# Ten stores of activation forms moved behind the seam of two products, and the three accumulation chains of a unit given their banks in another order

## The chip, the core and the metric

The kernel runs on one core of one Trainium2 chip. The metric is the device time of the program in microseconds (us): the median of several runs. The engines are PE (TensorE; its weight loads are shown as PEld), DVE (VectorE), ACT (ScalarE), POOL (GpSimd) and SP, whose queue issues nearly all DMAs. Each engine runs its instructions in their program order.

## The reference

One residual block for 512 tokens of width 2048, all in float32. What matters here is the MLP at its end:

```python
h2 = rmsnorm(x, g_mlp[l])
u = jax.nn.relu(jnp.einsum('bsd,df->bsf', h2, w_up[l]))     # 2048 -> 8192
x = x + jnp.einsum('bsf,fd->bsd', u * u, w_down[l])         # 8192 -> 2048
return rmsnorm(x, g_final)
```

Ahead of it stand an input projection, sixteen attention heads of two kinds and an output projection, which the change does not touch.

## The kernel before

Each float32 operand of a matmul is split into a high part (`hi`, a rounding cast on ACT, L63) and a low part (`lo`, a subtraction on DVE, L64); a product is hi x hi + hi x lo + lo x hi. Both products of the MLP are done block by block with seven block products in place of eight, numbered 1 to 7; sums and differences of blocks are formed on DVE.

**First product** (class `Unit`). `w_up` is worked through in 32 units of 256 columns. A unit has seven products of 16 matmuls each: eight that are 512 wide (L687) and eight that are 256 wide (L689). They accumulate in three PSUM chains of one bank each: A takes products 1, 6, 7 and 4, one on top of the other, B takes product 2, and C takes 5 and then 3. In the profile the chains are `psa`, `psb` and `psc`. After products 1, 6 and 7 ACT copies A out (L693, tiles `s`), and the next product of chain A waits for that copy. DVE adds chain B or C to a copy (L706 for B, L703 for C after product 7, L712 for C after product 3), and reads A once more after product 4 (L709 on ACT, L710 on DVE). From these come the unit's results, the tile `c`: two 256-wide halves by L700, relu and square by L714 and L715. Each unit's products 4 and 3 are issued among the next unit's.

The pool of the chains has two buffers for each of three tags, six banks in all. The tags get their banks in the order of their first use. When the first product is over, the pool is closed and two pools take the same six banks: the double-bank accumulators `accd` of the second product get the first four (the first accumulator the two banks of the first tag, the second those of the second tag), and `M1[1]` the last two.

**Stores.** Every two units share one tile `c`. Its seven forms are split and stored to DRAM (`store_form`, tiles `st`, 512 KB each, L722); four of them need one more DVE step first (L570 to L576). The list `todo` takes seven of them whenever a pair is done, and gives one back behind some of the products. Units 30 and 31 are not stored as forms: `store_last` stores their two parts each as they are (tiles `su`, L730). The buffers of `st` and `su` are a ring of three, which later serves for the residual (`xr`) too. What is left of `todo` after the last unit, and the four of `store_last`, are the list `jobs`.

**Second product** (`second`, `load_b`, `load_uf`). `w_down` is worked through in eight groups of units (the first two have three units each, the others four), each in two column halves `db`, each with seven products in the order 1, 5, 2, 6, 3, 7, 4. A product of the first group has 18 matmuls, 512 wide (L96 to L98): a split of 1024 columns (`wd` to `wh` and `wl`, or to `wx`) serves 12 of them, one of 512 columns six. Product 1 accumulates over all groups in `M1`; each other product ends in an accumulator `accd`, which ACT copies out in the first group (L786) and DVE adds to the sums `m` in the others (L788). The weights' blocks are combined on DVE first (L763 to L769). Product 1 of the first group is issued before the last unit's products 4 and 3.

The order on the engines is made when the program is built, by a scheduler that works with priorities and its own estimate of time: it moves an instruction ahead of others that would wait. `tc.issue_after(x)` forbids that an instruction is put ahead of `x`. Without it, the stores of `jobs`, which stand in the second group in the code, were put far ahead, between 1447 and 1465 us in the profile.

Of the kernel before, what the change touches and what calls it, by code (L numbers as in the profile page):

```python
# [8 lines left out]
F32 = mybir.dt.float32  # L9
# [5 lines left out]
P = 128  # L15
NT = 512
# [10 lines left out]
NU = DFF // P // 2  # L27
# [11 lines left out]
def block_kernel(ctx, tc, x, g_attn, w_in, b_f, g_out_sb, g_out_fox, w_out, g_mlp, w_up, w_down, g_final, y):  # L39
# [19 lines left out]
    lows, casts, loads = [None], [None], [None]  # L59
# [120 lines left out]
    with (  # L180
# [17 lines left out]
        def accumulate_v(c0, m, steps, prepare=None, more=None):  # L198

            per = NT // m  # L200
            banks = [acc.tile([P, NT], F32, tag="acc", name="accv") for _ in range(2 if more is not None else TB // per)]
            if more is not None:
                banks += [more.tile([P, NT], F32, tag="more", name="accm") for _ in range(2)]
            ps = [banks[t // per][:, t % per * m:(t % per + 1) * m] for t in range(TB)]
            k1, held = 0, []
            for j, step in enumerate(steps):
                k0, k1 = k1, k1 + step
                if prepare is not None:
                    prepare(k0, step)
                w = load_w([w_in[k0 * P:(k0 + step) * P, c:c + m // len(c0)].rearrange("(a p) c -> p a c", p=P) for c in c0],  # L210
                           step, m)
                held += [(k0 + i, w[i]) for i in range(step)]
                if prepare is None and j == len(steps) - 2:
                    continue
                for t in range(TB):
                    ts = slice(t * P, (t + 1) * P)
                    for k, wk in held:
                        mm3(ps[t], hH[:, k, ts], hL[:, k, ts], *wk, k == 0 and t % per == 0, k == KC - 1)
                    yield len(held) * 3 * (m / 2400 + 0.0133)
                held = []  # L220
            return ps

        def all_of(steps):
            while True:
                try:
                    next(steps)
                except StopIteration as e:
                    return e.value

        def out_product(n, mixed):  # L230
            ps = [acc.tile([P, NT], F32, tag="acc", name="acco") for _ in range(TB)]
            held = []
            for k0 in range(0, 2 * NH, 2):
                e0 = order[k0]
                w = load_w(w_out[e0 * P:(e0 + 2) * P, n * NT:(n + 1) * NT].rearrange("(a p) c -> p a c", p=P), 2, NT)
                ms = []
                for i in range(2):
                    ms.append(u_tile((k0 + i) % 4))
                    split(*ms[i], mixed[k0 // NH][:, (k0 + i) % NH, :])
                held += [(k0 + i, ms[i], w[i]) for i in range(2)]  # L240
                if n == 0 and k0 == 0:
                    continue
                for t in range(TB):
                    ts = slice(t * P, (t + 1) * P)
                    for k, m, wk in held:
                        mm3(ps[t], m[0][:, ts], m[1][:, ts], *wk, k == 0, k == 2 * NH - 1)
                    yield len(held) * 3 * 0.2267
                held = []
            return ps
# [131 lines left out]
        def v_columns(h):  # L381
            return 2 * WSB + h * P if h < NH else o0 + 2 * WSB + (h - NH) * P

        with tc.tile_pool(name="tr0", bufs=2, space=PSUM) as trp:
# [35 lines left out]
            ps = all_of(accumulate_v([v_columns(order[0])], 2 * P + NH, [1, 1] + [2] * 7, prepare, trp))  # L420
# [28 lines left out]
        with tc.tile_pool(name="attp", bufs=1, space=PSUM) as atp:  # L449
# [72 lines left out]
            for i in range(2 * NH):  # L522
                a = HEAD_AT[i]
                c = a + TURN + WEIGH if i != 2 * NH - 2 else VALUES_END + 3
# [28 lines left out]
    def form_parts(p, n):  # L553
        pair = F[p][n // 2][:, 2 * (n % 2):2 * (n % 2) + 2]
        return pair[:, :, 0, :], pair[:, :, 1, :]
# [25 lines left out]
    for n in range(4):  # L581
# [3 lines left out]
        ps = all_of(out_product(n, mixed)) if n else first_ps  # L585
# [38 lines left out]
    ups = ups_cm.__enter__()  # L624
# [11 lines left out]
    class Unit:  # L636
        def __init__(self, u):
            self.u = u
            first, last = (up_rows[i][:, :, 2 * u * P:2 * (u + 1) * P] for i in range(2))

            def blocks():
                return rw.tile([P, 2, KC // 2, P], F32, tag="rw", name="wu")

            def wide(src):
                raw = rw.tile([P, KC // 2, 2 * P], F32, tag="rw", name="wu")
                sp.dma_start(raw, src)
                return [raw[:, :, j * P:(j + 1) * P] for j in range(2)]

            if u == 0:
                b11, t1 = (wp.tile([P, KC // 2, P], F32, tag="wraw", name="wq") for _ in range(2))  # L650
                r = blocks()
                t2, t3 = r[:, 0], r[:, 1]
            else:
                r, q = blocks(), blocks()
                b11, t2, t1, t3 = r[:, 0], r[:, 1], q[:, 0], q[:, 1]
            sp.dma_start(b11, first[:, :, :P])
            self.raw = u not in early
            if self.raw:
                sp.dma_start(t1, first[:, :, P:])
                sp.dma_start(t3, last[:, :, P:])  # L660
                sp.dma_start(t2, last[:, :, P:])
            else:
                for t_, j in ((t1, 0), (t2, 2), (t3, 1)):
                    sp.dma_start(t_, td[u][:, j])
            b21, b22 = wide(last)
            self.b = {1: b11, 5: t1, 6: t2, 2: b21, 7: t3, 3: b22, 4: b21}
            self.A, self.B, self.C = (ups.tile([P, NT], F32, tag=c, name=f"ps{c}") for c in "abc")

        def product(self, p):
            if p == 2:  # L670
# [72 lines left out]
    def load_uf(p, group):  # L743
        uf[p] = form.tile([P, 2, group[1], 2 * P], F32R, tag=f"fh{UF_AT[p]}", name=f"uf{p}")
        sp.dma_start(uf[p].bitcast(F32), ufd[group][p])
# [67 lines left out]
    todo, sg = [], []  # L813
    old = None
    for u in range(NU + 1):
        new = Unit(u) if u < NU else None
        if u == NU - 1:
            for p in ORDER:
                load_uf(p, GROUPS[0])
            b_first = load_b(GROUPS[0], 0)  # L820
        if new is None:
            second(1, b_first, 0, GROUPS[0][1], True)
        for i, (who, p) in enumerate(((new, 1), (old, 4), (new, 5), (new, 6), (old, 3), (new, 2), (new, 7))):
            if who is None:
                continue
            who.product(p)
            if u == 0 and p == 6:

                for q in (4, 3):
                    a_form(q, hr, form_parts(q, 3), s12)  # L830
                xp_cm.__exit__(None, None, None)
                hx = ctx.enter_context(tc.tile_pool(name="hx", bufs=1, reuse_waits="tile"))
                more_parts.append(lambda: parts_at(hx, "hx"))
                sg_cm = tc.tile_pool(name="sg", bufs=1, reuse_waits="tile")
                sg.append(sg_cm.__enter__())
            if todo and i in (0, 2, 4, 5):
                store_form(*todo.pop(0))
            if p == 3 and who.u % 2 == 1 and who.u < NU - 2:
                todo += [(q, who.pair, who.u - 1) for q in A_ORDER]
        old = new  # L840
# [30 lines left out]
    jobs = [lambda a=a: store_form(*a) for a in todo] + [lambda u=u, h=h: store_last(u, h) for u in range(2) for h in range(2)]  # L871
    pieces = [(p, db) for db in range(2) for p in (2, 3, 7, 4)]
    spare = None
    for g, group in enumerate(GROUPS):
        last = g == len(GROUPS) - 1
        for db in range(2):
            if last and db == 1:
                in_w = lambda shape, name: wp.tile(shape, F32R, tag="wraw", name=name)
                last_hidden(0, in_w, in_w)
                last_weights(0, [lambda shape, name, i=i: spare.tile(shape, F32R, name=name) for i in range(2)])  # L880
            b = b_first if g + db == 0 else load_b(group, db)
            for i, p in enumerate(ORDER):
                if g + db + i:
                    second(p, b, db, group[1], g == 0)
                if db == 1 and not last:
                    load_uf(p, GROUPS[g + 1])
                if g == 1 and jobs and i % 2 == 0:
                    jobs.pop(0)()
                if g > 1 and pieces and i == 2:
                    add_residual(*pieces.pop(0))  # L890
        if g == 1:
            sg_cm.__exit__(None, None, None)
            spare = ctx.enter_context(tc.tile_pool(name="spare", bufs=1, reuse_waits="tile"))
# [105 lines left out]
```

## Time and profile before

| what | value |
|---|---|
| median of 3 runs | 2080.35 us (2078.67 to 2081.86) |
| profiled execution: time, span | 2080.91 us, 2079.2 us |
| granted clock of PE, mean | 0.998 |
| first product's units | from about 816 to 1452 us |
| seam of the two products | about 1437 to 1455 us |
| second product | to about 2031 us |

A profile's timeline row gives the start, the duration, the engine, the line in the kernel, the operation and its tiles, and in square brackets how long the engine sat idle before it and what it waited for. Matmuls are pipelined: one that is 512 wide is shown with 0.39 us, while the next starts 0.23 us after it. What a stretch costs is therefore read from starts. In a list of waits the three numbers are the sum in us, how often, and the longest.

### The profile page before, as it was taken

What the parts mean: (1) busy time and instruction counts of PE and PEld (TensorE: products, weight loads), DVE (VectorE), ACT (ScalarE), POOL (GpSimd) and SP (SyncE); (2) the same over time, 40 slices, a digit from 0 to 9 for tenths busy, and PEclk for the clock granted to TensorE, in tenths of its full rate; (3) what the DMA queues carried; (4) which work ended last, traced back from release to release, by engine and by line L of the source; (5) the groups of instructions that cost most, each with busy time, mean ns of one, the idle gap of its engine ahead of it and who ended that gap; (6) DMA issues with size and microseconds to landing.
All of it is one profiled execution on the core that took longest, in us unless ns stands there. A gap on an engine that the chain in (4) does not pass through costs nothing.

```text
span 2079.2 us, 26762 instructions
## 1 busy us (share of the span) xinstructions
PE 2055.9 (99%) x10292; PEld 1747.6 (84%) x10292; DVE 1601.8 (77%) x1827; ACT 1072.2 (52%) x1426; POOL 57.0 (3%) x77
## 2 busy tenths in 40 slices
PE   9999999999999999999999999999999999999998
PEld 8888888888888887888888888887888888888886
DVE  5747748748756657788988988989689989888885
ACT  6334334444446556566666666666644444443433
POOL 0000000001100000000000000000000000000003
PEclk9999999999999999999999999999999999999999
DMA  7947948937833445577778778778756764764732
GB/s 238 300 128 258 303 136 266 315 109 251 288 102 102 148 136 187 182 263 263 243 251 268 246 256 263 239 255 311 283 198 220 261 237 164 269 234 131 274 108 81
DMA packets 356575, 455.88 MB, mean 219 GB/s; under 512 B 11440, under 2 KB 255200, under 8 KB 347360
## 3 DMA queue, kind: packets, MB, share of 16 engines
q1 hardware_dynamic: 355488, 452.05, 65.7%
q10 hardware_dynamic: 960, 2.13, 0.3%
q8 instruction: 81, 1.33, 0.2%
q14 instruction: 46, 0.38, 0.0%
HBM read 347.17 MB, written 106.95 MB: 218 GB/s over the span
## 4 chain that ended last, share of the span: by engine, by line
PE 83%; DVE 7%; DMA 6%; issue 3%; ACT 1%; SPq 0%; DVEq 0%; ACTq 0%
PE accd L96 8%; PE accd L97 8%; PE accd L98 8%; PE psa L687 7%; PE accq L96 5%; PE accq L98 5%; PE accq L97 5%; PE psa L689 4%; PE psc L687 3%; DMA wu<-in_w_up_dram 3%; PE acco L97 3%; PE acco L98 3%; PE acco L96 3%; PE accv L96 3%; PE accv L97 2%
## 5 line engine op out<-in xcount | busy, mean ns | idle before, releaser
L63 ACT CAST wh<-wraw 128x1024 fp32r<-128x1024 f32 (+2 forms) x133 | 135.5, 1019 | 193.5 <-PE accq L97 114.8
L63 ACT CAST wh<-wd 128x1024 fp32r<-128x1024 f32 (+1 forms) x136 | 135.1, 1000 | 178.7 <-PE accd L98 120.6
L64 DVE TENSOR_TENSOR wl<-wraw,wh 128x1024 fp32r<-128x1024 f32 (+2 forms) x133 | 157.7, 1186 | 79.2 <-ACT wh L63 79.0
L64 DVE TENSOR_TENSOR wl<-wu,wh 128x1024 fp32r<-128x1024 f32 x166 | 202.0, 1223 | 15.8 <-PE psa L689 5.4
L63 ACT CAST wh<-wu 128x1024 fp32r<-128x1024 f32 x166 | 172.0, 1049 | 70.7 <-PE psa L687 26.1
L96 PE MATMUL accq<-hH,wh 128*128 128x512 f32 x512 | 201.1, 393 | 0.0
L98 PE MATMUL accq<-hH,wl 128*128 128x512 f32 x512 | 200.0, 391 | 0.0
L97 PE MATMUL accq<-hL,wh 128*128 128x512 f32 x512 | 199.7, 390 | 0.0
L64 DVE TENSOR_TENSOR wl<-wd,wh 128x1024 fp32r<-128x1024 f32 (+1 forms) x136 | 155.8, 1156 | 43.5 <-ACT wh L63 43.3
L96 PE MATMUL accd<-wh,uf 128*128 128x512 f32 x436 | 170.3, 391 | 3.2 <-DVE c L710 2.2
L98 PE MATMUL accd<-wh,uf 128*128 128x512 f32 x436 | 170.4, 391 | 0.0
L97 PE MATMUL accd<-wl,uf 128*128 128x512 f32 x436 | 170.3, 391 | 0.0
L63 ACT CAST wx<-wd 128x1024 fp32r<-128x1024 f32 (+1 forms) x88 | 87.7, 1000 | 121.7 <-PE accd L98 80.2
L64 DVE TENSOR_TENSOR wx<-wd,wx 128x1024 fp32r<-128x1024 f32 (+1 forms) x88 | 101.0, 1155 | 23.4 <-ACT wx L63 23.3
L98 PEld LDWEIGHTS accq<-hH,wl 128*128 128x128 f32 x512 | 96.1, 188 | 20.1
L97 PEld LDWEIGHTS accq<-hL,wh 128*128 128x128 f32 x512 | 96.2, 188 | 19.2
L96 PEld LDWEIGHTS accq<-hH,wh 128*128 128x128 f32 x512 | 96.2, 188 | 19.0
L788 DVE TENSOR_TENSOR m<-m,accd 128x1024 f32<-128x1024 f32 x84 | 102.4, 1219 | 10.8 <-PE accd L98 10.7
L97 PE MATMUL accd<-wx,uf 128*128 128x512 f32 x284 | 110.5, 389 | 0.0
L98 PE MATMUL accd<-wx,uf 128*128 128x512 f32 x284 | 110.5, 389 | 0.0
L96 PE MATMUL accd<-wx,uf 128*128 128x512 f32 x284 | 110.3, 389 | 0.0
L687 PE MATMUL psa<-fl,wh 128*128 128x512 f32 x388 | 105.9, 391 | 1.8 <-DVE fl L64 1.8
(288 smaller groups left out, 4860.8 us busy)
## 6 DMA issues: line engine op xcount, KB each, us to landing
ufd<-st SPq DMA_DIRECT2D x98, 512.0 KB, 6.1
wd<-in_w_down_dram SPq DMA_DIRECT2D x48, 1024.0 KB, 6.5
wraw<-in_w_in_dram SPq DMA_DIRECT2D x84, 512.0 KB, 5.0
uf<-ufd SPq DMA_DIRECT2D x42, 1024.0 KB, 7.0
sums<-in_w_up_dram SPq DMA_DIRECT2D x72, 512.0 KB, 6.0
td<-sums SPq DMA_DIRECT2D x24, 1536.0 KB, 8.0
wu<-td SPq DMA_DIRECT2D x71, 512.0 KB, 5.0
wu<-in_w_up_dram SPq DMA_DIRECT2D x32, 1024.0 KB, 7.5
```

The lines of the kernel that those rows point to most:

```text
L63: ins = casts[0] = act.copy(hi, src)
L64: lows[0] = dve.tensor_tensor(lo, src, hi.bitcast(F32), op=ALU.subtract)
L96: pe.matmul(out, sh, mh, start=first, stop=False, skip_group_check=True)
L97: pe.matmul(out, sh, ml, start=False, stop=False, skip_group_check=True)
L98: pe.matmul(out, sl, mh, start=False, stop=last, skip_group_check=True)
L687: pe.matmul(ps, hi[:, a, :], both, start=a == 0 and p in (1, 2, 5), stop=False, skip_group_check=True)
L689: pe.matmul(ps[:, :2 * P], lo[:, a, :], F[p][a // 4][:, a % 4, 0, :], start=False, stop=a == KC // 2 - 1, skip_group_check=True)
L788: dve.tensor_tensor(M[p][:, :, db, :], M[p][:, :, db, :], ps, op=ALU.add)
```

## The change

```diff
-            self.A, self.B, self.C = (ups.tile([P, NT], F32, tag=c, name=f"ps{c}") for c in "abc")
+            self.B, self.C, self.A = (ups.tile([P, NT], F32, tag=c, name=f"ps{c}") for c in "bca")
...
-            if todo and i in (0, 2, 4, 5):
+            if todo and u < NU - 1 and i in (0, 2, 4, 5):
                 store_form(*todo.pop(0))
...
-                if g == 1 and jobs and i % 2 == 0:
-                    jobs.pop(0)()
+                if g == 0 and jobs and db + i:
+                    with tc.issue_after(casts[0].ins), tc.issue_after(lows[0].ins):
+                        jobs.pop(0)()
```

It has three parts. The chains take their banks in the order B, C, A: chain A's banks go from 0 and 1 to 4 and 5, B's from 2 and 3 to 0 and 1, C's from 4 and 5 to 2 and 3. The last unit (`u` = 31) and the round behind it no longer store forms; of the last pair's seven forms six are left, so that `jobs` has ten stores where it had five. And `jobs` is worked off in the first group of the second product, one store behind each product from the second on (six in the first half, four in the second), where it was worked off in the second group. Each store's cast and subtraction now may not be put ahead of the cast and subtraction of the split that stands before it in the code.

The scheduler makes another order of it at the seam; behind the first group the order is the same again. Three places show it.

On PE, where the second product begins (its first matmul writes `m_0`, which is `M1[0]`); `fh_5662` and `fl_5663` are the forms that product 7 of the last unit reads, `fh_5652` and `fl_5653` those of product 2. With - and + as before and now:

```order
+L687 MATMUL psb<-fh_5652,wh 128x512 x4
+L687 MATMUL psb<-fl_5653,wh 128x512 x4
 L689 MATMUL psb<-fh_5652,wl 128x256 x4
 L689 MATMUL psb<-fl_5653,wl 128x256 x4
 L96 MATMUL m_0_6832<-wh,uf_12525 128x512
+L687 MATMUL psa<-fh_5662,wx 128x512 x4
+L687 MATMUL psa<-fl_5663,wx 128x512 x4
+L689 MATMUL psa<-fh_5662,wx 128x256 x4
+L689 MATMUL psa<-fl_5663,wx 128x256 x4
 L97 MATMUL m_0_6832<-wl,uf_12525 128x512
 L98 MATMUL m_0_6832<-wh,uf_12525 128x512
```

Product 7 stood behind 13 of the 18 matmuls of `m_0` and now stands behind the first of them; product 6 moves too, from behind product 2's 512-wide matmuls to ahead of the end of product 3 of unit 30.

On ACT, at the same place, before. `st` is a store's cast, `wd` a split of the second product, `wu` one of the first; the two copies from `psa` are those behind the last unit's products 6 and 7:

```order
L63 CAST st<-c 128x512 [waits DMAHW0_49,DVE_49]
L63 CAST st<-c 128x512 [waits DMAHW1_49]
L63 CAST wh<-wd 128x512 [waits DVE_49,PE_49]
L63 CAST st<-c 128x512 [waits DMAHW4_49]
L63 CAST wh<-wu 128x1024 [waits DVE_49,PE_49]
L693 COPY s_12642<-psa 128x512 [waits PE_49]
L714 ACTIVATE c<-c 128x1024 [waits DVE_49]
L715 ACTIVATE c<-c 128x1024 [waits Activation_49]
L63 CAST wx<-wu 128x1024 [waits PE_49]
L63 CAST wh<-wd 128x1024 [waits DVE_49]
L693 COPY s_12719<-psa 128x512 [waits DVE_49]
```

And now:

```order
L63 CAST wh<-wd 128x1024 [waits DMAHW6_49,PE_49,Activation_49]
L63 CAST wh<-wd 128x512 [waits PE_49]
L693 COPY s_12633<-psa 128x512 [waits PE_49]
L63 CAST wh<-wu 128x1024 [waits DVE_49,PE_49,Activation_49]
L714 ACTIVATE c<-c 128x1024 [waits DVE_49]
L715 ACTIVATE c<-c 128x1024 [waits Activation_49]
L63 CAST wx<-wu 128x1024 [waits PE_49]
L693 COPY s_12701<-psa 128x512 [waits DVE_49]
L63 CAST wh<-wd 128x1024 [waits PE_49]
L63 CAST wh<-wd 128x512 [waits PE_49]
L63 CAST st<-c 128x512 [waits DMAHW1_49]
```

Three stores' casts have left the stretch, and the copy behind product 7 stands directly behind one cast instead of two.

On ACT in the first group, now (the stores' casts wait for a buffer of the ring, DMAHW, and the copies L786 free an accumulator):

```order
L63 CAST st<-c 128x512 [waits DMAHW4_49,DVE_49]
L63 CAST wh<-wd 128x512 [waits PE_49,Activation_49]
L786 COPY m_12913<-accd 128x2x512 [waits PE_49]
L63 CAST wh<-wd 128x1024 [waits DMAHW0_49,Activation_49]
L63 CAST st<-c 128x512 [waits DMAHW6_49,DVE_49]
L63 CAST wx<-wd 128x512 [waits PE_49,Activation_49]
L63 CAST su<-c 128x512 [waits DMAHW0_49]
L786 COPY m_12945<-accd 128x2x512 [waits PE_49]
```

Before, this stretch held splits and copies alone. On DVE the stores' subtractions and the four extra steps move along with the casts: of the eight stores that stood between the first store of the last pair and L710, one is left. L703 behind the last unit's product 7 stood behind two splits, and now stands behind one. On SP's queue the stores stand among the loads of `wd` for the first group's second half and for the second group.

## The prediction

> **What bounds the kernel now.** The first view is the page's part 1.
>
> ```profile
> PE 2055.9 (99%) x10292; PEld 1747.6 (84%) x10292; DVE 1601.8 (77%) x1827; ACT 1072.2 (52%) x1426; POOL 57.0 (3%) x77
> ```
>
> PE is busy for all but 23.3 us of the 2079.2 us span, so a change that leaves PE's work as it is can only win PE's pauses and the stretches in which its clock is low. The next view, busy time in stretches, shows whether there are any where the change works: the two rows around the seam between the first product and the second, and the one behind them.
>
> ```profile
> 1393.00:1420.00 27.00, 26.82 (x156) 23.52 (x155) 22.23 (x28) 16.17 (x21) 0.00 (x0) 1.00 0.92 296
> 1420.00:1455.00 35.00, 31.13 (x171) 26.36 (x170) 32.78 (x42) 23.05 (x32) 0.00 (x0) 1.00 0.89 317
> 1455.00:1500.00 45.00, 45.00 (x193) 37.04 (x193) 30.71 (x32) 27.83 (x33) 0.00 (x0) 0.96 0.75 266
> ```
>
> The columns are the stretch, its length, the busy time of PE, PEld, DVE, ACT and POOL, PE's granted clock, the DMA share and GB/s. From 1420 to 1455 PE lacks 3.87 us while DVE has work for 32.78 of 35 us; behind it the clock is 0.96. This seam holds a sixth of all of PE's idle time. What ended those pauses is in the list of PE's waits:
>
> ```profile
> PE accd L96 <- DVE c L710: 2.2, 1, 2.2
> PE psa L687 <- ACT s L693: 1.6, 2, 1.4
> PE psc L687 <- DVE s L703: 0.3, 1, 0.3
> ```
>
> Three results that others deliver late: a copy on ACT, and two additions on DVE. PE's timeline places them, and gives what they cost in starts rather than in busy time.
>
> ```profile
> 1426.28 1.09 PE L687 MATMUL psa<-fh,wh 128*128 128x512 f32 x4
> ...
> 1429.07 1.09 PE L687 MATMUL psc<-fh,wh 128*128 128x512 f32 x4
> ...
> 1437.43 0.40 PE L96 MATMUL m<-wh,uf 128*128 128x512 f32 x1
> ...
> 1437.90 0.39 PE L98 MATMUL m<-wh,uf 128*128 128x512 f32 x1
> ...
> 1440.18 0.39 PE L96 MATMUL m<-wh,uf 128*128 128x512 f32 x1
> 1440.53 1.19 PE L687 MATMUL psa<-fh,wx 128*128 128x512 f32 x4
> ...
> 1446.16 1.19 PE L687 MATMUL psa<-fh,wh 128*128 128x512 f32 x4 [1.40 <-ACT s L693]
> ...
> 1449.46 1.20 PE L687 MATMUL psc<-fh,wx 128*128 128x512 f32 x4 [0.26 <-DVE s L703]
> ...
> 1454.74 0.50 PE L96 MATMUL accd<-wh,uf 128*128 128x512 f32 x1 [2.21 <-DVE c L710]
> ...
> 1457.99 0.63 PE L98 MATMUL accd<-wh,uf 128*128 128x512 f32 x1
> ...
> 1463.27 0.39 PE L96 MATMUL accd<-wx,uf 128*128 128x512 f32 x1
> ```
>
> The undisturbed pace: one product of a unit (16 matmuls) takes 1429.07 - 1426.28 = 2.79 us, and a matmul of the second product (1440.18 - 1437.90)/10 = 0.228 us. Against that pace the seam loses four terms. (a) From 1437.43 to 1446.16 stand 18 matmuls of product 1 of the second product and chain A's product 7: 18 x 0.228 + 2.79 = 6.89 us of work in 8.73 us, **1.84 us lost**. (b) Product 4 takes 1449.46 - 1446.16 = 3.30 us, **0.51 lost**. (c) Product 3 and the pause behind it take 5.28 us, **2.49 lost**. (d) The 30 matmuls from 1454.74 to 1463.27 take 8.53 us where 6.84 is the pace, **1.69 lost**: nine of them last up to 0.63 us and stand 0.43 us apart. Together 6.53 us, 0.31% of the run. The rest of PE's idle time lies at other places, which the change does not touch.
>
> **Term (a), the copy of A.** Product 4 adds into the bank that product 7 filled, so it waits for ACT's copy of it. ACT's timeline:
>
> ```profile
> 1438.43 0.62 ACT L63 CAST st<-c 128x512 fp32r<-128x512 f32 x1 [3.90 <-DMA ufd<-st]
> ...
> 1439.90 0.58 ACT L693 COPY s<-psa 128x512 f32<-128x512 f32 x1
> ...
> 1443.63 1.05 ACT L63 CAST wx<-wu 128x1024 fp32r<-128x1024 f32 x1 [1.10 <-PE psa L689]
> 1444.59 1.04 ACT L63 CAST wh<-wd 128x1024 fp32r<-128x1024 f32 x1
> 1445.54 0.58 ACT L693 COPY s<-psa 128x512 f32<-128x512 f32 x1
> ```
>
> A store's cast stood 3.90 us for a transfer to give its buffer back, with everything of ACT behind it: the copy of A after product 6 came at 1439.90, and product 7 could start only then, behind 13 of the 18 matmuls. Only five were left to cover ACT's work behind product 7 (cast 1.05, cast 1.04, copy 0.58). In the changed order ACT has no store there, product 7 stands behind the first of the 18, and the other 17 lie between products 7 and 4: 17 x 0.228 = 3.88 us. ACT then needs one cast and the copy, 1.05 + 0.58 = 1.63 us. The wait goes with 2.2 us to spare. Product 6 is moved as well, ahead of product 2's 16 matmuls and the rest of product 3 (about 3.4 us), which covers the copy that product 7 needs. I take the whole 1.84.
>
> **Terms (b) and (c), DVE.** Its timeline ahead of the last pause:
>
> ```profile
> 1440.29 0.68 DVE L706 TENSOR_TENSOR s<-s,psb 128x512 f32<-128x512 f32 x1
> ...
> 1446.46 1.22 DVE L64 TENSOR_TENSOR wx<-wu,wx 128x1024 fp32r<-128x1024 f32 x1
> 1447.59 1.22 DVE L64 TENSOR_TENSOR wl<-wd,wh 128x1024 fp32r<-128x1024 f32 x1
> 1448.73 0.68 DVE L703 TENSOR_TENSOR s<-s,psc 128x512 f32<-128x512 f32 x1
> 1449.32 0.69 DVE L64 TENSOR_TENSOR wl<-wd,wh 128x512 fp32r<-128x512 f32 x1
> 1449.92 0.69 DVE L64 TENSOR_TENSOR st<-c,st 128x512 fp32r<-128x512 f32 x1
> 1450.53 0.42 DVE L700 TENSOR_TENSOR c<-s 128x256 f32<-128x256 f32 x1
> 1450.86 1.76 DVE L765 TENSOR_TENSOR wd<-wd 128x1536 f32<-128x1536 f32 x1
> 1452.53 1.23 DVE L64 TENSOR_TENSOR wl<-wd,wh 128x1024 fp32r<-128x1024 f32 x1
> 1453.66 0.69 DVE L64 TENSOR_TENSOR su<-c,su 128x512 fp32r<-128x512 f32 x1
> 1454.26 0.42 DVE L710 TENSOR_TENSOR c<-c,psa 128x256 f32<-128x256 f32 x1
> ```
>
> For (b), L703 frees chain C for product 3. Two splits of 1.2 us ran between the copy (done at 1446.12) and L703; now L703 stands directly behind one split, and the copy comes about 1.6 us behind product 7 instead of 2.7, with 17 matmuls and product 4 in between. All 0.51 go. For (c), the second product's first accumulator took chain A's banks, which L710 reads last. In the other order of the banks it gets chain B's, whose last reader L706 ran 14 us before the pause. All 2.49 go, unless the operands are late: their split now stands directly behind L703, and product 3 covers it with 2.79 us.
>
> What is late next: the second accumulator now has chain C's banks, and waits for L712, which follows product 3. It is wanted 18 x 0.228 = 4.10 us behind product 3's end. From L703's end DVE has in between a split of 1.23, L700 0.42, a split of 0.69, a store's 0.69, L765 1.76, a split of 1.23, L710 0.42 and L712 itself, as long as L703: 7.1 us. Product 3 and the first accumulator give 2.79 + 4.10 = 6.9 us, and L703 can be done a cast, a split and itself behind product 7 (1.05 + 1.23 + 0.68 = 3.0 us), which is 3.7 us ahead of product 3. That leaves 3.5 us; if DVE has other work first, 0 or less. I take 0 for this wait, with 1 us as the other end.
>
> **Term (d), the clock.** Two rows of the stretches view:
>
> ```profile
> 818.00:822.00 4.00, 2.23 (x13) 1.64 (x12) 4.00 (x7) 4.00 (x11) 0.00 (x0) 1.00 0.93 267
> 1455.00:1458.00 3.00, 3.00 (x9) 2.28 (x9) 3.00 (x6) 0.01 (x1) 0.00 (x0) 0.52 1.04 423
> ```
>
> At 818 PE idles 1.77 of 4 us once, and the granted clock stays 1.00. At the seam it idles 1.4, 0.26 and 2.21 us within 11 us, and then the clock is 0.52. So the dip belongs to the sum of the pauses or to the last one; with (a) to (c) gone neither is there, and I take all 1.69.
>
> The Trainium skill ("TensorE: Matmul & The Clock Gate", section "Why this matters for your kernels") puts the limit at idle gaps over about 3 us. By that rule the 2.21 us pause would not have halved the clock, and the dip need not go with it; the sum would be 4.84 instead of 6.53. Here the dip starts with the first matmul behind that pause, so the trace speaks against the rule taken as a sharp limit.
>
> **What is added: ten stores in the first group of the second product.** Nothing is computed that was not computed before. A store is a cast on ACT (0.62), a subtraction on DVE (0.69) and a 512 KB transfer; four of the ten have one more DVE step of 0.69. The first group's 14 products take 14 x 4.10 = 57.4 us on PE. DVE's own work there is 14 x (1.23 + 0.69) + 8 x 1.76 = 41.0 us; all ten stores add 14 x 0.69 = 9.7: 50.7 of 57.4. ACT has 14 x (1.05 + 0.62) + 12 x 1.02 = 35.6 and gets 6.2. Both fit, hidden behind PE. So do the transfers: the same bytes as before move between 1420 and 1500, where the share is (35 x 0.89 + 45 x 0.75)/80 = 0.81; in 6 us less that is 0.88. What can still hurt is the ring of three store buffers, because a store's cast stands in ACT's queue ahead of splits and of the copies that free an accumulator.
>
> ```profile
> 1464.83 1.02 ACT L786 COPY m<-accd 128x1024 f32<-128x1024 f32 x1 [0.73 <-PE accd L98]
> ufd<-st SPq DMA_DIRECT2D x11, 512.0 KB, 8.7
> 1439.80 10.62 DMA ufd<-st
> ```
>
> The first row is such a copy, the second the stores' median from issue to landing between 1400 and 1500 us, the third the longest in the chain there. One store per product means that a buffer must be back after 3 x 4.10 = 12.3 us. Cast, subtraction and 8.7 us make 10.0, and with 10.62 it is 11.9: in time both ways, by little. On SP's queue a load of the next weights that stands behind a store waits for a DVE step just behind that store's subtraction, so it is hardly held. I put all this at 0.4 us, with 0 and 2 as ends. POOL has no part in it.
>
> **The sum.** 1.84 + 0.51 + 2.49 + 1.69 - 0.4 = 6.1 us. The profiled run took 2080.91 us (span 2079.2 and 1.7 around it), so 2074.8 for it; the median of the three runs is 0.56 lower, which gives **2074.3**.
>
> **Rivals.** *A new wait in part.* The second accumulator waits its 1 us, the store ring takes 2, and PE pauses enough that a dip of 1.69 stays. Gain 6.53 - 1 - 2 - 1.69 = 1.8, time 2078.5. For it: slacks of only 1 to 2 us. Against it: each needs an unfavourable end. *The stalls were DVE's, not the stores'.* DVE is at 32.78 of 35 us; if the moved work comes back at the seam as the same lateness of L703 and L712, only (a) goes: 2078.5 as well. Against it: of the eight stores that stood there behind the first, seven leave, with all four extra steps, 11 x 0.69 = 7.6 of DVE's 32.78 us. *The clock dip alone stays*, as the skill's limit would allow: 2080.35 - 6.1 + 1.69 = 2075.9. *The change does not do what it says*: the order of work shows the stores gone from the seam, except one in front of it and one behind it, so I give this nothing beyond noise.
>
> *Slower.* The place is ACT's queue in the first group, the mechanism the ring of three. If a store lands in L us, stores follow each other every (L + 1.3)/3 us instead of 4.1; seven of the ten stand behind a full ring, and about 2.5 us of slack comes first (4.1 less the copy's 1.02 and the cast's 0.62). The loss is 7 x ((L + 1.3)/3 - 4.1) - 2.5 us: from L = 14.7 it eats the whole gain, at 16.5 it is 10.3 us and the time 2084.6. Against it: 8.7 us was measured with the transfers near full share, and 10.62 is the longest.
>
> **How the numbers follow.** Forecast with most of the 6.5 us: 0.64; the dip alone stays: 0.08; a new wait in part, or DVE late again: 0.20; slower: 0.08, half of it by more than 0.2%. A measurement of this kernel can tell about 0.2%, 4.2 us, from no change. The first case and most of the second are faster by more: 0.69. Slower by more 0.04, the rest 0.27. The low end takes all 6.53 us and 1.3 us of scatter (the three runs span 3.2 us): 2072.5. The high end takes in the partial cases with their scatter: 2080.0; above it lie the slower case and a few unlucky partial ones.
>
> **What would show it.** In the new profile the stretch around the seam has PE busy throughout and a granted clock of 1.00; L710 and the copy of A are gone from PE's waits; ACT's casts of stores wait for landings between 1450 and 1490 instead of before 1450, without PE waiting for L786 or for a split. I am wrong if PE waits for L712, for L786 or for a split in the first group, if the clock is still low behind the seam, or if the stores land later than 12 us after issue.

## The result, and the profile after the change

| | before | after |
|---|---|---|
| median, runs | 2081.24 us, 8 (2078.67 to 2083.44) | 2074.76 us, 8 (2072.54 to 2078.12) |
| profiled execution: time, span | 2080.91, 2079.2 | 2075.16, 2073.1 |
| PE's granted clock, mean | 0.998 | 0.999 |

The ratio is 0.9969, 95% interval 0.9960 to 0.9978: faster by 0.31%, 6.5 us (4.6 to 8.3 by the interval). The forecast was 2074.3 us.

The stretches view of the changed kernel, with the columns as in the prediction:

```profile
1393.00:1420.00 27.00, 27.00 (x157) 23.85 (x157) 22.82 (x29) 16.52 (x21) 0.00 (x0) 1.00 0.95 305
1420.00:1455.00 35.00, 35.00 (x193) 30.43 (x192) 31.36 (x38) 22.23 (x29) 0.00 (x0) 1.00 0.83 283
1455.00:1500.00 45.00, 45.00 (x200) 37.29 (x199) 35.70 (x41) 32.49 (x43) 0.00 (x0) 1.00 0.87 309
```

PE is busy for all of 35 us where it lacked 3.87, the clock is 1.00 behind the seam, and DVE and ACT have most of the ten stores behind 1455 (35.70 and 32.49 us there in place of 30.71 and 27.83). PE's timeline, the same places as before:

```profile
1429.78 1.09 PE L687 MATMUL psc<-fh,wh 128*128 128x512 f32 x4
...
1438.16 0.40 PE L96 MATMUL m<-wh,uf 128*128 128x512 f32 x1
...
1445.06 1.07 PE L687 MATMUL psa<-fh,wh 128*128 128x512 f32 x4
...
1447.83 1.09 PE L687 MATMUL psc<-fh,wx 128*128 128x512 f32 x4
...
1450.62 0.40 PE L96 MATMUL accd<-wh,uf 128*128 128x512 f32 x1
...
1457.45 0.39 PE L96 MATMUL accd<-wx,uf 128*128 128x512 f32 x1
```

No row has a pause in brackets. Term by term, against the pace that the prediction took: (a) 1445.06 - 1438.16 = 6.90 us for 6.89 of work; (b) 2.77; (c) 2.79; (d) 6.83 for 6.84. All four are zero. From the first row to the last it is 27.67 us, where it was 1463.27 - 1429.07 = 34.20: **6.53 us less**. ACT and DVE show how late the others now are:

```profile
1441.38 1.05 ACT L63 CAST wx<-wu 128x1024 fp32r<-128x1024 f32 x1 [0.82 <-PE psa L689]
1443.23 0.59 ACT L693 COPY s<-psa 128x512 f32<-128x512 f32 x1 [0.79 <-DVE c L700]
```

```profile
1444.24 0.68 DVE L703 TENSOR_TENSOR s<-s,psc 128x512 f32<-128x512 f32 x1
...
1450.48 0.42 DVE L710 TENSOR_TENSOR c<-c,psa 128x256 f32<-128x256 f32 x1
1450.82 0.69 DVE L712 TENSOR_TENSOR s<-s,psc 128x512 f32<-128x512 f32 x1
```

The copy of A is done at 1443.82, 1.2 us ahead of product 4, where the forecast had 2.2: the row's bracket shows that it also stood 0.79 us for DVE's L700, which the forecast left out; L703 at 1444.92, 2.9 us ahead of product 3; L712 at 1451.51, while the second accumulator is wanted 4.10 us behind 1450.62, at 1454.72: 3.2 us of slack where the forecast had 3.5. L710 itself ends at 1450.90, 0.28 us behind product 3; in the new order of the banks the first accumulator does not wait for it. The DMA view gives the ten stores' issue to landing between 1440 and 1500 us:

```profile
ufd<-st SPq DMA_DIRECT2D x6, 512.0 KB, 5.8
usd<-su SPq DMA_DIRECT2D x4, 512.0 KB, 4.7
```

Before, the prediction's 8.7 was the median of eleven such stores between 1400 and 1500 us, ten of them issued by 1440.

### The profile page after: what moved, and what is told of

Read it like the earlier page. It is cut to its first block, busy times and chain, and to the rows that moved or that the text cites. A ratio compares the mean times of both kernels' runs of the same rounds, so it can differ in the third digit from the quotient of the medians.

```text
span 2073.1 us, 26761 instructions
## 1 busy us (share of the span) xinstructions
PE 2053.1 (99%) x10292; PEld 1746.6 (84%) x10292; DVE 1601.9 (77%) x1827; ACT 1071.9 (52%) x1426; POOL 57.1 (3%) x77
## 4 chain that ended last, share of the span: by engine, by line
PE 90%; DVE 4%; DMA 3%; issue 2%; ACT 1%; SPq 0%; ACTq 0%; DVEq 0%
PE psa L687 9%; PE accd L96 8%; PE accd L98 8%; PE accd L97 8%; PE accq L96 5%; PE accq L98 5%; PE accq L97 5%; PE psa L689 5%; PE psc L687 4%; PE acco L97 3%; PE acco L98 3%; PE acco L96 3%; PE accv L96 3%; PE accv L97 3%; PE accv L98 3%; PE psc L689 2%
```

## The experiments

The yardstick is the stretch on PE from product 3 of unit 30 to the 49th accumulator matmul (the first `accd<-wh` behind the first block of `wx`). It takes in every place of the seam, and a profile shows it to 0.1 us, while the runs of one kernel scatter by 5 us and more (31 runs of the kernel before: 2078.2 to 2086.9). Before it is 38.28 us, after 31.75. It is one execution's figure each time.

**The two parts of the change, one at a time.** Only the banks:

```diff
-self.A, self.B, self.C = ( ... for c in "abc")
+self.B, self.C, self.A = ( ... for c in "bca")
```

> Only the other order of the banks; stores and every engine's order as before the change. Theory (four separate terms): the copy of A after product 6 stays late, so (a) 1.84 us and (b) 0.51 us stay; the first accumulator starts at product 3's end, so (c) 2.49 us goes. If the half clock belongs to the last pause or to the sum of the pauses, (d) 1.69 us goes as well. New: the first accumulator's copy L786 stands in ACT's queue behind L709, L714 or a split that waits for DVE's late L700, which can hold the accumulator that follows by up to 1.8 us. From the first product 3 matmul of unit 30 to the first accd<-wx matmul: 34.20 - 2.49 - 1.69 + (0 to 1.8) = 30.0 to 31.8 us; time 2.4 to 4.2 us less than before. Rival (the pauses are one budget of DVE's, which only moves): the second accumulator waits for L712 what the first no longer waits, and the stretch stays at 33 us or more, gain under 1.5 us. Rival on the clock: it drops behind the 1.4 and 0.26 us pauses alone, and (d) stays: 31.7 us or more.

Measured: ratio 0.9993 (0.9985 to 1.0002), by itself not to be told from no change. The stretch is 35.97 us, 2.31 less. PE's timeline, its pauses:

```profile
1445.14 1.19 PE L687 MATMUL psa<-fh,wh 128*128 128x512 f32 x4 [1.41 <-ACT s L693]
1448.64 1.20 PE L687 MATMUL psc<-fh,wx 128*128 128x512 f32 x4 [0.46 <-DVE s L703]
1461.32 0.50 PE L96 MATMUL accd<-wx,uf 128*128 128x512 f32 x1 [1.42 <-ACT m L786]
```

(a) and (b) stay, (c) and (d) go, and L786 costs 1.74 us in their place: ACT stood 3.85 us at L714 for DVE's late L700 with that copy behind it. The expectation's stretch ended ahead of this pause (30.15 us there); with it the gain is 2.3, under its lower figure of 2.4.

Only the stores, the banks as before ("abc"):

> The stores as after the change, the banks in the order of before. Theory: (a) and (b) go, since they are the stores'. L710 ended in the changed kernel about 0.3 us behind product 3's end, so the first accumulator waits 0.2 to 0.6 us for it in place of 2.21, and a pause that short leaves the clock at 1.00: the stretch from product 3 of unit 30 to the first accd<-wx is 27.67 + 0.4 = 28.1 us (27.9 to 28.4), gain about 6.1 us. By it the order of the banks is worth 0.4 us once the stores are gone. Rival (the terms are independent, as the prediction's sum has them): without the banks' order (c) 2.49 stays and (d) with it, the stretch is 31 to 32 us, gain 2.4 us.

Measured: ratio 0.9975 (0.9966 to 0.9985). The short stretch is 28.09 us, the long one 32.17, 6.11 less than before. The one pause left:

```profile
1453.14 0.50 PE L96 MATMUL accd<-wh,uf 128*128 128x512 f32 x1 [0.16 <-DVE c L710]
```

The short stretch is where the theory had it (27.9 to 28.4), against the 31 to 32 of independent terms. So in these profiles the stores alone are worth 6.1 and the banks alone 2.3, and both together 6.5. (Against the second execution of before, below, it is 5.6, 1.8 and 6.0; the times do not tell the stores alone from both, their intervals overlap.) With the stores gone the banks' order is worth 0.42: L710 is late because of the stores, and both edits treat that one lateness.

**Place in the code, or the guard.** Without `tc.issue_after`:

> As after the change, but without the guard that forbids that a store is put ahead of the split in front of it; the stores' code stands in the first group as in the changed kernel, the banks in its order too. Theory: the place in the code does nothing by itself; the scheduler puts stores back into the seam, the copy of A is late again, and the run is that of the banks alone: stretch 30 to 32 us, gain 2.4 us (1 to 4). Rival: the stores' place in the first group is what helps, and the gain is 5 us or more.

Measured: ratio 0.9997 (0.9989 to 1.0006); stretch 34.18 us. The stores are back ahead of the split they stood behind, as the theory said, but in another order than before: (a) to (d) are zero, the copy of A is not late, and the stretch that the expectation means is 27.64 us and not 30 to 32. What is lost comes behind it. The new pause has the mechanism of the prediction's slower rival in small: a store's cast waits for a landing ahead of the copy that frees an accumulator. On ACT, and then on PE:

```profile
1465.13 0.62 ACT L63 CAST su<-c 128x512 fp32r<-128x512 f32 x1 [1.48 <-DMA ufd<-st]
1465.65 1.01 ACT L786 COPY m<-accd 128x1024 f32<-128x1024 f32 x1
```

```profile
1466.71 0.50 PE L96 MATMUL accd<-wx,uf 128*128 128x512 f32 x1 [2.14 <-ACT m L786]
```

The stretch says 4.1 us of gain, the times 0.6 (-1.2 to 2.3); the profiled execution, 2083.77 us, is the slowest of the eleven. A second execution:

> The run without the guard once more, to see what its seam does in a second execution: its times gave 0.6 us of gain, its profiled execution 4.1 us at the seam. What is measured: from the first matmul of product 3 of unit 30 to the first matmul of the accumulator that follows the first wx block (the 49th accumulator matmul), 38.3 us before, 31.7 after, 34.2 in the first profile of this kernel. Theory A (the stores put back into the seam stall ACT by whatever the transfers then take, so the seam differs from run to run): 34 to 38 us, with another wait of a store's cast for a landing than the 1.33 and 1.48 us of the first, and with a dip of the clock where the pause for L786 is over 2.2 us. Theory B (the seam is the same each time, and the first product ahead of it was slow in most runs by chance): 34.0 to 34.4 us again.

Measured: stretch 35.49 us, a pause of 1.88 us for L786 and a half clock behind it. That is inside theory A's range and outside theory B's. But the store's cast stood 1.12 us for its landing in place of 1.48, so the pause is the shorter one; the stretch is longer for the half clock alone, which theory A expected behind pauses over 2.2 us. The rest lies ahead of the seam: product 3 of unit 30 starts at 1435.41 and 1434.63 us here, at 1429.07 before, and between 816 and 1420 us PE idles 6.95 and 7.51 us against 2.78. The stores there wait longer for landings, though the engines' order is that of before up to unit 30. Why this build does so stays open. At the seam the guard is what keeps PE from pausing: 34.18 and 35.49 us without it, 31.75 with it in both executions of the changed kernel; of the 5.4 us that the times lose without it (2080.12 against 2074.76) this is a part.

Before, with the guard alone on its five stores:

> As before the change, with the guard alone: the five stores of the list stay in the second group, five of the last pair's stay at the seam, among them the one that ACT waited for; banks as before. Theory: (a) stays, since the ring of three is still full when that store's cast comes; DVE has five stores less ahead of L703 and L710, so (b) goes and (c) shrinks to 0.5 to 1.5 us, and the clock stays up: stretch 29.7 to 31 us, gain 3.2 to 4.5 us. Rival (it is all one lateness of the stores): as long as the first stores stand there nothing is won, stretch over 33 us.

Measured: ratio 0.9981 (0.9972 to 0.9990), stretch 33.92, 4.36 us less. PE's order at the seam is that of before, and a store's cast still stood 3.82 us for a landing, so the theory had (a) at 1.84. It is 1446.90 - 1439.42 - 6.89 = 0.59. (b), which was to go, is 0.83, (c) 0.65 and (d) 0.1. The gain of 4.4 us lies in the forecast range of 3.2 to 4.5 because the two misses partly offset each other. ACT behind product 7:

```profile
1445.31 1.05 ACT L63 CAST wh<-wd 128x1024 fp32r<-128x1024 f32 x1 [0.73 <-DVE wd L763]
1446.27 0.58 ACT L693 COPY s<-psa 128x512 f32<-128x512 f32 x1
```

One cast stands ahead of the copy, where the prediction's rows have two of 1.05 us. So the wait for the landing does not make (a) by itself; the second cast behind product 7 does the larger part. The prediction's own rows agree. PE's order puts product 7 behind the 13 matmuls in any case, and it starts at 1440.53, 0.12 us behind their end (1440.18 + 0.228). ACT has caught up before product 7 ends: it stands 1.10 us for that, until 1443.63. So the landing made 0.1 us of (a), and the order of the casts the rest.

**The kernels before and after once more.**

> The kernel before once more. The same stretch was 38.3 us in the profile on which the prediction rests. If the seam's four terms are a property of the order (ACT's store meets a full ring whenever it comes), 37 to 39 us again with the same three waits (a copy of A, L703, L710) and a dip behind the last; if the 3.90 us wait for a landing was one execution's, (a) is under 1 us and the stretch under 37.

> The changed kernel once more: the stretch was 31.7 us without a pause and PE had 2.2 to 3.5 us of slack in each of the waits, so 31.6 to 31.9 again and no pause between 1425 and 1500 us; a pause there would mean that the first profile was a lucky one.

Measured: after 31.75 us again, without a pause. Before 37.75, with these:

```profile
1444.88 1.19 PE L687 MATMUL psa<-fh,wh 128*128 128x512 f32 x4 [1.40 <-ACT s L693]
...
1449.47 0.73 PE L687 MATMUL psc<-fh,wx 128*128 128x512 f32 x2 [1.54 <-DVE s L703]
...
1454.74 0.50 PE L96 MATMUL accd<-wh,uf 128*128 128x512 f32 x1 [2.22 <-DVE c L710]
```

Its stretches view behind the last pause:

```profile
1455.00:1458.00 3.00, 3.00 (x14) 2.43 (x14) 3.00 (x6) 0.00 (x1) 0.00 (x0) 1.00 1.02 413
```

The same waits, (b) 1.80 where it was 0.51, and after a pause of 2.22 us **no dip**: 1.00, where the prediction's row had 0.52 after 2.21. The pauses here add up to 5.16 us, more than the 3.87 of the first execution. So term (d) is neither the sum of the pauses nor the length of the last alone.

**What halves the clock.** One pause by itself, in the changed kernel; the second kernel has 512 columns in place of 128:

```diff
+            if new is None and p == 3:
+                flat = uf[5].rearrange("p a u c -> p (a u c)")
+                for s in range(1):
+                    part = flat[:, 0:128]
+                    dve.scalar_tensor_tensor(part, who.m6[:, 0:128], 0.0, part.bitcast(F32), op0=ALU.mult, op1=ALU.add)
```

> The changed kernel with one more DVE instruction behind product 3 of the last unit: it rewrites 128 columns of the form that the first accumulator's first matmul reads (adds zero times the tile s), so that PE pauses once, at the first accumulator, with no other pause in the 20 us ahead. In the changed kernel L700, behind which it stands on DVE, started at 1452.69 and the last matmul of product 3 ended at 1450.78: a single pause of 2.4 to 2.7 us. If the half clock of the kernel before belongs to the length of the last pause alone (2.21 us there, against a single 2.14 without a dip in the run without the guard), the limit lies between 2.14 and 2.21 and the clock drops here: nine or so matmuls 0.43 us apart, 1.7 us lost beside the pause. If it belongs to the sum of pauses close together (1.40 + 0.26 + 2.21 = 3.87 us before), or to a limit of about 3 us as the Trainium skill has it (TensorE: Matmul & The Clock Gate, section Why this matters for your kernels), the clock stays at 1.00 and the matmuls behind the pause stand 0.23 us apart.

> As the short single pause, with 512 columns rewritten: the pause is about 0.5 us longer, 2.8 to 3.2 us. Length of the last pause alone: dip of 1.7 us. Sum of pauses: 3.0 is less than 3.87, so by it no dip is needed, but the limit of the sum is not known and lies between 2.14 and 3.87. Limit of about 3 us on a single pause: on the edge, either way.

Measured, in one run each: pauses of 2.62 and 3.02 us, both with a half clock. It starts 0.3 us behind the first, and 0.8 us before the end of the second. The stretches view of the one with 2.62, then of the one with 3.02:

```profile
1454.00:1457.40 3.40, 3.40 (x10) 2.62 (x9) 2.98 (x3) 1.71 (x2) 0.00 (x0) 0.50 0.45 185
```

```profile
1453.20:1460.00 6.80, 6.02 (x14) 4.80 (x15) 4.09 (x5) 2.93 (x4) 0.00 (x0) 0.50 0.49 196
```

The half clock lasts 3.4 us, or twice that. The other runs show the same 3.4 us wherever it dips before PE's work is over, and that equal pauses at one place differ. At 818 us, between the attention and the first product, the kernel of the stores alone:

```profile
820.59 0.73 PE L687 MATMUL psa<-fl,wh 128*128 128x512 f32 x2 [1.77 <-DVE fl L64]
```

```profile
818.00:822.00 4.00, 2.23 (x13) 1.68 (x12) 4.00 (x7) 4.00 (x10) 0.00 (x0) 0.97 0.92 280
822.00:825.00 3.00, 3.00 (x13) 2.69 (x13) 2.90 (x8) 2.94 (x7) 0.00 (x0) 0.50 1.12 381
```

The same pause of 1.77 us, which left the clock at 1.00 in the prediction's row of before, here halves it from 821.8 to 825.2. Over all profiled executions, from 20 us on, none of 59 pauses of 1.00 to 1.68 us is followed by a dip; of thirteen of 1.75 to 2.22 us five are and eight are not; the two longer ones are. So no length between 2.14 and 2.21 is a limit, as the expectation would have had it; nor is a sum of pauses, since 2.62 alone was enough and 5.16 was not. The Trainium skill ("TensorE: Matmul & The Clock Gate", section "What's actually happening") says that the clock is set by activity in a free-running window of 3413 ns. The dips of 3.4 us agree. The traces show the windows too. Every execution has one more half clock at its end, behind PE's last matmul, here in the first of the kernel before:

```profile
2069.55:2072.96 3.41, 0.29 (x2) 0.00 (x0) 1.62 (x6) 1.13 (x4) 1.19 (x1) 1.00 0.16 65
2072.96:2076.37 3.41, 0.00 (x0) 0.00 (x0) 1.23 (x3) 1.33 (x2) 0.00 (x0) 0.50 0.51 195
```

In the seven executions with an earlier dip, that dip starts a whole number of times 3.4133 us ahead of this one, to 0.01 us: here 2072.96 - 1455.14 = 617.82, 181 times; in the others 366, 206, 179, 331, 182 and 181 times. So in each execution the windows can be counted back from its end. The 1.77 us at 818 before then fall into two windows, 1.25 and 0.52, the 2.22 of its second execution 1.06 and 1.16, the 2.14 without the guard 1.09 and 1.05; none of these dips. The 2.21 before, in 1451.73 to 1455.14, and the 1.77 above, in 818.35 to 821.77, lie whole in one, and the next window is at half clock. Over all 14 executions there are 8415 windows at full clock from 20 us on. All 20 with 1.766 us or more of PE's idle time are followed by a half clock; of the others one is, at 1.760, while 1.745 and 1.764 are not. So a dip needs about 1.76 us of idle time, a little over half a window, inside one window, and for a pause of 1.8 to 3.5 us it is chance where a border falls. As an estimate from these figures: a pause of 2.21 us escapes when a border leaves less than 1.76 on both sides, 1.31 of 3.41 us, so it dips in about six executions of ten, and term (d) is worth about 1.0 us on average. Behind the 3.02 us pause the second window has only 0.79 us of idle time and the clock stays down; it is the only dip in the midst of PE's work with idle time in its first window, and why it stays open.

The same page's limit of about 3 us ("Why this matters for your kernels"), which the prediction weighed, does not hold here as a sharp limit: 1.76, 1.77 and 1.88 us were enough. By that rule (d) would have been 0.

**The ring of three store buffers.** One or two of the three are held through the first group:

```diff
+    kept = [wp.tile([P, 2, NT], F32, tag="wraw", name="kept") for _ in range(1)]
...
+        if g == 0:
+            for t_ in kept:
+                pool.tensor_tensor(t_[:, 0, :8], M[4][:, 0, 1, :8], M[4][:, 0, 1, :8], op=ALU.add)
```

> The changed kernel with one of the three store buffers held back through the first group of the second product, so that the ten stores have a ring of two. By the prediction's formula with the landing of 5.8 us that the changed kernel shows, stores follow each other every (5.8 + 1.3)/2 = 3.55 us, under the 4.10 of a product: no loss, time as changed within 0.2%; with the longest landing of 8.1 it would be 4.7 us, 0.6 us too late for single stores, which the slack of 2.5 us covers. Rival (the landing under load is nearer the 8.7 us of before, since the ring also paces the loads): (8.7 + 1.3)/2 = 5.0, loss 8 x 0.9 - 2.5 = 4.7 us.

> The changed kernel with two of the three store buffers held back through the first group, so that each store waits for the landing of the one before. By the prediction's formula a store every 5.8 + 1.3 = 7.1 us in place of 4.1: 9 x 3.0 - 2.5 = 24 us more than the changed kernel, with PE waiting for L786 copies and splits behind the casts in ACT's queue. Rival (the stores are not on PE's path, since ACT's splits run ahead and only the stores themselves get late): under 5 us more.

Measured with two: ratio 0.9980 (0.9971 to 0.9990), the seam clean (31.75), the time 0.1% over the changed kernel's ratio, inside the 0.2% expected. ACT's casts wait up to 2.11 us for landings, and PE waits for none of that; it loses 1.66 us at 1509.5, where loads of `wd` were late. They stand on SP's queue behind `xr`, a load that takes its buffer from the same ring, so this cost is in part the experiment's. With one: the time was 2080.25 us in one run, and the ten casts stand from 1446.6 to 1512.0, (1511.97 - 1446.56)/9 = 7.27 us apart, near the formula's 7.1, though only six of them stood for a landing. In pauses PE loses 2.9 us over the first group and the start of the second, and not 24; two of them:

```profile
1461.15 0.50 PE L96 MATMUL accd<-wx,uf 128*128 128x512 f32 x1 [1.41 <-ACT m L786]
1473.86 0.50 PE L96 MATMUL accd<-wh,uf 128*128 128x512 f32 x1 [0.17 <-ACT m L786]
```

The scheduler, which knew of the smaller ring, put the stores further apart and splits and copies ahead of them. So the rival, under 5 us, is nearer; the one time is 5.1 us over the changed kernel's profiled execution. The formula's step from late stores to a late PE, with ACT's order fixed, was not tried.

**The guard on all stores**, those of the first product's units as well:

> The changed kernel with the guard on the stores of the first product's units as well, so that none of them is put ahead of the split before it in the code. What there is to win: between 816 and 1420 us PE of the changed kernel idles 3.1 us, each time because a store's cast stood in ACT's queue waiting for a landing; at most these go, 3 us or 0.15%. Theory (the guard is a remedy for stores put too early, wherever they are): idle from 816 to 1420 under 1.5 us and a time 1 to 3 us below the changed kernel. Rival (there the ring is full because two of three stores follow each other in the code, whatever their exact place, or the scheduler's other order opens new pauses): idle of 2.5 us or more, time not below the changed kernel's, or above it.

Measured: ratio 0.9980 (0.9971 to 0.9989), against 0.9969 (0.9960 to 0.9978) for the changed kernel; PE idles 3.86 us between 816 and 1420, against 3.07 and 4.46 in the two executions of the changed kernel, and the stretch is 32.31. The rival holds, by its second reason. The guard did take away most of ACT's waits for landings there: 12.3 us in ten, where the changed kernel's profile has 46.3 in twenty. But few of those were on PE's path. Of the changed kernel's 3.07 us of idle time only 1.34 stand behind a store's cast, and 1.6 lie at 816 to 823, ahead of any store; so the expectation's "each time" was wrong, and at most 1.3 us was to be won. In exchange the new order has a pause of its own, with a half clock behind it. A store's cast stands for a split's subtraction, with the copy of A behind it; on ACT, and then on PE:

```profile
937.49 0.62 ACT L63 CAST st<-c 128x512 fp32r<-128x512 f32 x1 [1.94 <-DVE wl L64]
...
938.97 0.56 ACT L693 COPY s<-psa 128x512 f32<-128x512 f32 x1
```

```profile
939.59 0.73 PE L687 MATMUL psa<-fh,wx 128*128 128x512 f32 x2 [2.20 <-ACT s L693]
```

No run beat the changed kernel.

## Why the prediction was right, and where its steps were not

- **The sum.** 6.53 us of loss at the seam, all of which goes: shown, to 0.1 us, in the profiled executions. The whole execution gained 5.75 us; 0.7 of the seam's was given back by pauses ahead of it, which scatter (PE idles 2.4 to 7.5 us between 816 and 1420 over the runs). In the second execution of before the seam's loss is 6.0 us, with other sizes and no half clock. That the time came within 0.5 us of the forecast is in part luck: the runs of one kernel scatter by ten times that, and a term of 1.69 that is not always there was added in full.
- **(a) 1.84 and (b) 0.51.** Both go by the stores alone. The prediction put (a) first to the 3.90 us wait for a landing, and said that product 7 could start only then; by its own rows that wait made 0.1 us, and the guard on the five stores left such a wait while two thirds of (a) went. Its other half, two casts ahead of the copy with five matmuls to cover them, was right. The sizes are one execution's: 1.58 and 1.80 in the second.
- **(c) 2.49, put down to the banks.** The size was right and the credit was not. With the banks alone 2.4 go at that place and 1.74 come back at L786, since L700 stays late; with the stores alone all but 0.3 of it go. L710 was late because of the stores.
- **(d) 1.69, "the sum of the pauses or the last one".** That it goes with the pauses was right. That it is part of the kernel's time in every run was wrong: the second execution of before hasn't got it. It goes by the idle time inside one window of 3.41 us.
- **The second accumulator's wait for L712**, taken as 0: 3.2 us of slack.
- **The ten stores, 0.4 (0 to 2).** Mis-sized, 0: the landings took 5.8 and 4.7 us in place of the 8.7 they were priced with, most likely because the row of before came from the stretch that crowds them (ten of its eleven stores were issued between 1400 and 1440 us). For the same reason the store casts' waits for landings between 1450 and 1490, which were to be seen, are not there.
- **Rivals.** "The stalls were DVE's" falls with the stores-only run, though the count against it is off by one: behind the first store seven stood ahead of L710 and six left, with the four extra steps 10 x 0.69 = 6.9 us of DVE's work and not 7.6; "the dip alone stays" falls since a dip needs a pause; the slower one needed 14.7 us to land. Its mechanism does exist, 1.48 us long, in the run without the guard.

## What to carry to other kernels

When several waits at one seam come from one late engine, price the edits together: what each saves alone doesn't add up (6.1 and 2.3 made 6.5). A store moved in the code stays where a scheduler wants it unless its order is pinned, and a pin that cures one place can open a pause in another. A long wait of one engine costs nothing as long as no wait of the bottleneck ends on it. Read a stretch that you hope to win from two executions, and count a clock dip as a chance, not as a term.

## What the runs showed of the hardware

A PE pause of about 1.75 to 2.2 us halves the clock in some executions and not in others (1.77 us at 818: 0.50 behind it in one kernel, 1.00 in two with the same order there; 2.21 and 2.22 us: 0.52 and 1.00). What decides is whether about 1.76 us of idle time falls inside one of the windows of 3.41 us, which run on through the whole execution. The half clock lasts 3.4 us and costs 1.7 us; with the 3.02 us pause it lasted 6.8. The same order of stores also lands differently from execution to execution: in the thirteen that keep that order in the first product, ACT waited between 39.5 and 51.7 us in all for landings there, in twenty waits each time.
